# Earlier projections for head pairs and evenly spaced splits of the output weights in a hybrid attention and DeltaNet step

## The chip, the cores and the metric

The kernel runs on one core of one Trainium2 chip. What is compared is the device time of one execution in microseconds (us). The engines are TensorE (PE, matmuls; PEld is its weight load), VectorE (DVE), ScalarE (ACT), GpSimd (POOL) and SyncE (SP), which issues nearly all DMAs here. Each engine works through its own instructions in program order and waits on semaphores for the others.

## What is computed

Two layers of a mixer run over 1280 tokens (256 prompt tokens and 1024 sample tokens) with 1024 features. In each layer one input projection feeds two branches: latent attention with 8 heads, and a gated DeltaNet with 4 heads and one scan per direction. Their gated outputs are joined and go through one output projection. What matters here is the attention branch:

```python
q = jnp.einsum('bsr,rf->bsf', rmsnorm(q_lat, q_a_norm), w_qb)...   # 8 heads of 64 + 32
kv = jnp.einsum('bsr,rf->bsf', ckv_all, w_kvb)...                  # 1536 keys for the sample tokens
s = (jnp.einsum('bqhd,bkhd->bhqk', qn, k_nope)
     + jnp.einsum('bqhr,bkr->bhqk', qp, k_pe)) * scale
p = jax.nn.softmax(s, axis=-1)
o = jnp.einsum('bhqk,bkhd->bqhd', p, v)
...
out = jnp.einsum('bse,ed->bsd', jnp.concatenate([o_a, o_b], axis=-1), w_out)
x = x + gate * out
```

The 256 prompt tokens attend to themselves; the 1024 sample tokens attend to themselves and 256 cached keys.

## The kernel before

**A planner sets the order.** The kernel is written as some forty Python generators ("threads"), each with a priority from the table `PR`. While the kernel is built, `Sched.run` repeatedly takes the operation that can start first by a model of engine clocks and latencies, and among equals the one with the smaller priority number. What it takes is the program order of that engine. A thread stops at `yield "name"` until another thread has set the flag of that name (`sd.flag`), which happens in program order, not in time. Where the model sees PE idle for longer than about a microsecond, `keep_warm` puts in dummy matmuls (line 436, tile `spare`). Nearly all instructions are recorded at one helper line, L315, so they are told apart by their tiles.

**Attention, one layer.** The stage begins while the last DeltaNet heads still run.

- `proj(p)` (p = 0 to 3) makes the queries and keys of heads 2p and 2p+1: three `kp` matmuls of 512 keys, then six `qp` matmuls, all plain fp32. Each result is copied by ACT, its remainder is taken by DVE, and both halves go to DRAM (`kx_d`, `qx_d`). At its end it loads the next pair's weights. Before it begins, it waits for `rest` (the right-hand buffers are open), for `proj{p-1}`, and for tile 5 of head 2p-2.
- `loads(h)` reads head h's keys and queries back from DRAM through SP. Keys have two buffers (`Kt[h % 2]`), so the four pieces wait for tiles 0, 4 and 8 of head h-2 and for its end; queries have three (`Qh[h % 3]`) and wait for the end of head h-3.
- `prep(h)` finds the largest score of each query: 26 `pm` matmuls in two PSUM banks, each reduced by DVE, then a small maximum, a transpose (`mxt`), and a row that goes through DRAM (`mx_d`) into the queries. `pace` holds its parts back to tiles 1 and 6 of head h-2 and tiles 0 and 2 of head h-1.
- `main` works through the heads. For each key tile it issues the score matmuls `sp` (three for 512 queries: high by high, high by low, low by high), ACT takes the exponential into `pe`, and two tiles later `pv` multiplies with the values (`po`). POOL, and for two tiles of a head DVE, adds up the `pe` tiles; one pair of `pd` matmuls makes the denominators from the sum. Head h needs `prep{h}`. The flag `m{h}.{i}` is set when main reaches sample key tile i (0 to 9) of head h, `main{h}` at its end. A head has 66 `sp` matmuls: 6 of 256 columns for the prompt, 60 of 512.
- `vproj(p)` makes the values of a pair (`vp`).

**Output weights.** `pre_c` starts when the last DeltaNet head is done. It loads the output weights in 16 pieces (`wor`, 128 x 512, six buffers), and `split_wo` splits each into a rounded high part (ACT, `woh`) and a remainder (POOL, `wol`). After the last split it opens the pool for the output stage (`load_c`, `mm_thread`, matmuls `wop`), which begins when head 7 has left its prompt block.

Of the kernel before, what the change touches and what calls it, by code (L numbers as in the profile page):

```python
# [16 lines left out]
P = 128  # L17
# [7 lines left out]
NK = T + PAST  # L25
DEPTH = 2
HA = 8
# [370 lines left out]
def body(tc, I, O):  # L398
# [8 lines left out]
    def open_pool(stack, name, bufs=1, **k):  # L407
        return Pool(stack.enter_context(tc.tile_pool(name=name, bufs=bufs, **k)), bufs)
# [8 lines left out]
    def bank(name):  # L417
        yield "bank"
        Sched.banks.remove(min(Sched.banks))
        t = pp.pool.tile([P, 512], F32, tag="mm", name=name)  # L420
        Sched.span(t)
        return t

    def free(t):
        Sched.push(lambda: Sched.banks.append(Sched.after(max(Sched.wr[t.name] + Sched.rd[t.name]), "PE")))
# [138 lines left out]
    def mixer(l, hhl):  # L564
        sd = Sched()
# [803 lines left out]
        def split(x, n):  # L1369

            i = at["evn"] = at.get("evn", -1) + 1
            ev = at["ev"][i % len(at["ev"])]
            S.copy(ev[:, 0, :n], x)
            (V if x.space == PSUM else G).tensor_tensor(ev[:, 1, :n], x, ev[:, 0, :n].bitcast(F32), op=ALU.subtract)
            return ev[:, :, :n].bitcast(F32)

        def proj(p):
            ckv, qn, hw = at["ckv"], at["qn"], at["hw"]
            if p:
                yield "rest"  # L1380
                yield f"proj{p-1}"
                yield f"m{2*p-2}.5"
            for k0 in range(0, NK, 512):
                pt = yield from bank("kp")
                PE.matmul(pt, hw[:, 2, :], ckv[:, k0 : k0 + 512])
                yield 0
                SY.dma_start(kx_d[p, :, :, k0 : k0 + 512], split(pt, 512))
                free(pt)
            for c0, n in BLK:
                pt = yield from bank("qp")  # L1390
                for k in range(2):
                    PE.matmul(pt[:, :n], hw[:, k, :], qn[:, k, c0 : c0 + n], start=(k == 0), stop=(k == 1))
                yield 0
                SY.dma_start(qx_d[p, :, :, c0 : c0 + n], split(pt[:, :n], n))
                free(pt)
            if p + 1 < HA // 2:
                SY.dma_start(hw, I["w_hd"][l, p + 1])
            yield 0
            sd.flag(f"proj{p}")
# [295 lines left out]
        def pre_c():  # L1695
            yield f"done{HB-1}"
            yield "rest"
            gs.close()
            b2 = open_pool(bs, f"b2{l}", bufs=1, side="right")
            for t in ("ob", "rc"):  # L1700
                at[t].append(b2.tile([P, 512], F32, tag=t, name=t))
            cw = open_pool(cs, f"cw{l}", bufs=1)
            xs_ = ExitStack()
            cx = open_pool(xs_, f"cx{l}", bufs=1)
            yield 0
            for e in range(8):
                hi = cw.tile([P, DM], F32R, tag=f"woh{e}", name=f"woh{e}")
                lo = cw.tile([P, DM], F32R, tag=f"wol{e}", name=f"wol{e}")
                wo.append((hi, lo))
                for hf in range(2):  # L1710
                    raw = cx.tile([P, 512], F32, tag="wor", name="wor", bufs=6)
                    sl = slice(hf * 512, hf * 512 + 512)
                    SY.dma_start(raw, I["w_out"][l, e * P : (e + 1) * P, sl])
                    wor.append((hi[:, sl], lo[:, sl], raw))
                    yield 0
                    if len(wor) >= 6:
                        split_wo(wor.pop(0), e)
            while wor:
                split_wo(wor.pop(0), len(wor) // 2)
                yield 0  # L1720
            xs_.close()
            c0 = open_pool(cs, f"c0{l}", bufs=1)
            cc_[0] = c0
            load_gate(0, c0)
            for t in range(2):
                sq[t] = c0.tile([P, 2], F32, tag=f"sq{t}", name="sq")
            sd.add(PR['ldc'], load_c())
            sd.add(PR['mm'], mm_thread())

        wor = []  # L1730

        def split_wo(w, e):
            hi, lo, raw = w
            S.copy(hi, raw)
            (V if len(wor) % 2 < VWO else G).tensor_tensor(lo, raw, hi.bitcast(F32), op=ALU.subtract)
# [14 lines left out]
        def load_c():  # L1750
            for t in range(NT):
                if t == 1:
                    yield f"main{HA-2}"
                    yield f"vv{HA//2-1}"
                    yield f"prep{HA-1}"
                    m1 = at["t1"].rearrange("p (a b) -> p a b", a=4)
                    x, of, cc_["tm"] = m1[:, 0], m1[:, 1].rearrange("p (a b) -> p a b", a=8), m1[:, 2]
                elif t == 2:
                    yield "tm0"
                    yield "C"  # L1760
                if t >= 3:
                    yield f"fin{t-3}"
                if t != 1:
                    x = cc_[0 if t % 3 == 0 else 1].tile([P, DM], F32, tag="x", name="x", bufs=1 if t % 3 == 0 else 2)
                SY.dma_start(x, (I["x"] if l == 0 else xs)[t * P : (t + 1) * P, :])
                if t == 0:
                    yield "attn0"
                    n1 = hp.tile([P, 4, 8, P], F32R, tag="hl1", name="n1")
                pool = cc_.get(t % 2)
                if t != 1:  # L1770
                    of = pool.tile([P, 8, P], F32, tag="of", name="of")
                SY.dma_start(of, o_d[:, :, t * P : (t + 1) * P].rearrange("e p t -> p e t"))
                if t >= 2:
                    yield f"mm{t-2}"
                if t < 2:
                    oh, ol = n1[:, 2 * t], n1[:, 2 * t + 1]
                else:
                    oh, ol = [cc_[1].tile([P, 8, P], F32R, tag=f"o{i}{t%2}", name=f"o{i}") for i in "hl"]
                V.tensor_copy(oh, of)
                G.tensor_tensor(ol, of, oh.bitcast(F32), op=ALU.subtract)  # L1780
                yield 0
                xt[t], ot[t] = x, (oh, ol)
                sd.flag(f"ld{t}")

        def load_gate(t, pool):
            gb[t] = pool.tile([P, DM], F32, tag="gbc", name="gbc", bufs=1)
            SY.dma_start(gb[t], gate_d[l, t // 2 : t // 2 + 1, :].to_broadcast([P, DM]))
# [25 lines left out]
        def mm_thread():  # L1813
            for t in range(NT):
                yield f"ld{t}"
                oh, ol = ot[t]
                x = xt[t]
                if t < 2:
                    s2[t], jk = sq[t], cc_[0].tile([P, 512], mybir.dt.bfloat16, tag="jk", name="jk")
                else:  # L1820
                    s2[t], jk = [cc_[1].tile([P, n], d, tag=f"s{n}", name=f"s{n}", bufs=3 if n == 2 else 1) for n, d in ((2, F32), (512, mybir.dt.bfloat16))]
                for hf in range(2):
                    pt = yield from bank("wop")
                    cs = slice(hf * 512, hf * 512 + 512)
                    for e in range(8):
                        for i, (a, w) in enumerate(((oh, wo[e][0]), (oh, wo[e][1]), (ol, wo[e][0]))):
                            PE.matmul(pt, a[:, e, :], w[:, cs], start=(e == 0 and i == 0), stop=(e == 7 and i == 2))
                        yield 0
                    if t == 1:
                        tm = cc_["tm"][:, cs]  # L1830
                    elif t:
                        tm = cc_[1].tile([P, 512], F32, tag="tm", name="tm", bufs=2)
                    else:
                        tm = cc_[0].tile([P, 512], F32, tag="of", name="tm0")
                    with sd.side(1):
                        V.tensor_tensor(tm, pt, gb[0 if t < 2 else 2][:, cs], op=ALU.mult)
                        free(pt)
                        V.tensor_tensor(x[:, cs], x[:, cs], tm, op=ALU.add)
                        S.activation(jk, x[:, cs], AF.Square, accum_out=s2[t][:, hf : hf + 1])
                        if hf:  # L1840
                            sd.add(PR['fc'], fin(t))
                    if not t and hf:
                        sd.flag("tm0")
                sd.flag(f"mm{t}")
# [124 lines left out]
```

## Time and profile before

| | |
|---|---|
| median of 3 runs | 2251.47 us (2249.32 to 2253.87) |
| the profiled execution | 2246.48 us |
| its span, first to last instruction | 2244.3 us |
| PE busy | 2101.7 us, 94% of the span |
| DVE, POOL, ACT busy | 64%, 38%, 33% of the span |
| mean granted TensorE clock | 0.98 |
| dummy matmuls (`spare`) | 271 instructions, 542 records |

A matmul on plain fp32 leaves two records in the trace, one on the rounded type `fp32r` leaves one. Matmuls overlap in the pipeline, so a record of 0.4 us may begin 0.23 us after the one before; the distance of the starts is what a matmul costs PE. A stretch of the span is named below by its start and end in us. The stretches are cut at the first score matmul of a head, or of a key tile, by counting `sp` records.

### The profile page before, as it was taken

Reading aid. Unit: us, or ns where it says so; the run is one execution under the profiler, and the core shown is the slowest. Engines: PE = TensorE matmul, PEld = TensorE weight load, DVE = VectorE, ACT = ScalarE, POOL = GpSimd, SP = SyncE. Lnnn points to the kernel's source line nnn. Section 1 sums busy time; section 2 is a strip of 40 time slices with the busy share of each in tenths; the row PEclk is TensorE's granted clock in tenths of the full one; section 3 lists DMA queues with packets and bytes.
Section 4 is the critical chain, followed back from the end, with each engine's and each line's share of the span. In section 5 each row is a group of like instructions: output and inputs, shape, how many; then the busy total and the mean of one; then the engine's idle time right before and its main releaser. Section 6 shows DMA issues by size and latency. Waiting matters only on the chain.

```text
span 2244.3 us, 35296 instructions
## 1 busy us (share of the span) xinstructions
PE 2101.7 (94%) x12158; PEld 1570.2 (70%) x12158; DVE 1438.6 (64%) x3105; ACT 739.7 (33%) x2052; POOL 858.1 (38%) x741
## 2 busy tenths in 40 slices
PE   8899999989898998999999999998999899899998
PEld 6677777778575655665777887787876666566586
DVE  4766577775855564563667675987668657456454
ACT  4244224322223344423222441433222333442311
POOL 2343214342414246446331551324252334653721
PEclk9999999999999999999999999999999999999999
DMA  7476777776593736232423655667868573633143
GB/s 272 133 238 186 247 229 223 207 219 217 191 270 120 201 88 183 78 80 62 139 100 94 192 174 153 192 215 211 257 230 244 157 202 88 191 103 79 46 159 108
DMA packets 413091, 380.33 MB, mean 169 GB/s; under 512 B 91585, under 2 KB 334241, under 8 KB 412657
## 3 DMA queue, kind: packets, MB, share of 16 engines
q1 hardware_dynamic: 412912, 378.07, 56.4%
q8 instruction: 97, 1.59, 0.3%
q14 instruction: 82, 0.66, 0.1%
HBM read 246.82 MB, written 131.15 MB: 168 GB/s over the span
## 4 chain that ended last, share of the span: by engine, by line
PE 41%; DVE 15%; DMA 12%; issue 3%; POOL 3%; SPq 3%; ACT 2%; DVEq 0%; POOLq 0%; ACTq 0%
PE wop L315 9%; PE sp L315 7%; PE po L315 6%; PE zp L315 6%; DVE at L315 3%; SPq L315 3%; PE pm L315 2%; DVE wtmp L315 2%; DVE W L315 2%; POOL pe L315 2%; DVE yc L315 2%; DMA at<-kx_d 1%; PE px L315 1%; DMA wr<-in_w_main 1%; DMA qx_d<-at 1%
## 5 line engine op out<-in xcount | busy, mean ns | idle before, releaser
L315 PE MATMUL zp<-hh,wh 128*128 128x512 f32 (+2 forms) x1128 | 423.3, 375 | 10.5 <-DVE wh L315 5.4
L315 PE MATMUL zp<-hl,wh 128*128 128x512 f32 (+2 forms) x1128 | 422.2, 374 | 4.3 <-POOL hl L315 4.2
L315 PE MATMUL zp<-hh,wl 128*128 128x512 f32 (+2 forms) x1128 | 420.8, 373 | 4.7 <-POOL wl L315 4.7
L315 POOL TENSOR_TENSOR pe<-pe,pe 128x1024 f32<-128x1024 f32 x112 | 267.5, 2388 | 283.3 <-PE po L315 213.4
L315 POOL TENSOR_TENSOR wl<-wr,wh 128x512 fp32r<-128x512 f32 (+1 forms) x118 | 161.6, 1371 | 404.8 <-DVE wh L315 231.3
L315 ACT ACTIVATE pe<-sp 128x512 f32<-128x512 f32 (+1 forms) x336 | 196.7, 589 | 216.2 <-PE sp L315 197.9
L315 DVE TENSOR_REDUCE at<-pm 128x1 f32<-128x512 f32 (+1 forms) x336 | 210.1, 682 | 67.3 <-PE pm L315 66.5
L315 PEld LDWEIGHTS zp<-hh,wh 128*128 128x128 f32 (+1 forms) x1128 | 214.7, 190 | 47.7 <-DVE wh L315 6.9
L315 PEld LDWEIGHTS zp<-hl,wh 128*128 128x128 f32 (+1 forms) x1128 | 214.8, 190 | 39.0 <-issue 6.6
L315 PEld LDWEIGHTS zp<-hh,wl 128*128 128x128 f32 (+1 forms) x1128 | 214.4, 190 | 39.3 <-POOL wl L315 7.3
L315 PE MATMUL sp<-at 97*128 97x512 f32 (+1 forms) x572 | 196.3, 400 | 1.2 <-DVE ob L315 0.9
L315 PE MATMUL sp<-at,at 97*128 97x512 f32 (+1 forms) x484 | 186.9, 410 | 1.3 <-ACT vv L315 0.9
L315 PE MATMUL po<-pe,vv 128*64 128x512 f32 (+1 forms) x704 | 163.0, 578 | 0.3 <-ACT pe L315 0.2
L315 POOL TENSOR_SCALAR kpt<-ktok,kdb 128x128 f32<-128x128 f32 x160 | 130.7, 829 | 65.7 <-DMA ai_d<-kpt 55.5
L315 PEld LDWEIGHTS sp<-at 97*128 97x128 f32 x572 | 103.8, 190 | 35.6 <-issue 16.6
L315 DVE TENSOR_TENSOR wtmp<-blk,W 104x31 f32<-104x31 f32 (+15 forms) x248 | 107.2, 432 | 27.5 <-POOL W L315 15.2
L315 PEld LDWEIGHTS sp<-at,at 97*128 97x128 f32 x484 | 91.5, 190 | 34.7 <-issue 11.3
L315 DVE SCALAR_TENSOR_TENSOR yc<-zp_sb,cwh,yc 128x256 f32<-128x256 f32 (+1 forms) x144 | 103.6, 719 | 4.1
L315 PE MATMUL wop<-woh,ol 128*128 128x512 f32 x256 | 101.9, 398 | 1.6 <-POOL ol L315 1.6
L315 PE MATMUL wop<-woh,oh 128*128 128x512 f32 x256 | 102.0, 398 | 0.0
L315 PE MATMUL wop<-wol,oh 128*128 128x512 f32 x256 | 101.9, 398 | 0.0
L315 DVE RECIPROCAL rc<-rc 128x128 f32<-128x128 f32 x80 | 70.0, 920 | 47.7 <-ACT rc L315 47.6
(287 smaller groups left out, 3938.5 us busy)
## 6 DMA issues: line engine op xcount, KB each, us to landing
wr<-in_w_main SPq DMA_DIRECT2D x120, 256.0 KB
ti<-ai_d SPq DMA_DIRECT2D x144, 192.0 KB
ai_d<-ai SPq DMA_DIRECT2D x80, 256.0 KB
kc<-kqv_d SPq DMA_DIRECT2D x160, 128.0 KB
wa<-in_w_ada SPq DMA_DIRECT2D x64, 256.0 KB
kqv_d<-yc SPq DMA_DIRECT2D x48, 256.5 KB
kx_d<-at SPq DMA_DIRECT2D x22, 512.0 KB
kq<-kqv_d SPq DMA_DIRECT2D x16, 641.0 KB
```

The costliest lines, as they stand in the source:

```text
L315: op = Op(lambda: f(*a, **k), self.key, self.ns(name, a, k, aps), outs, [x for x in aps if x is not acc])
```

## The change

`proj(p)` for p = 2 and 3 now waits for tile 0 of head 2p-3 where it waited for tile 5 of head 2p-2, and `proj(1)` waits for no tile at all. `pre_c` waits before each split for a turn: `turn` lists every other key tile of heads 0 to 6, finds at its first call how many of them main has passed, and from there gives one tile to each split.

```diff
@@ -1379,7 +1379,8 @@
             if p:
                 yield "rest"
                 yield f"proj{p-1}"
-                yield f"m{2*p-2}.5"
+                if p > 1:
+                    yield f"m{2*p-3}.0"
             for k0 in range(0, NK, 512):
                 pt = yield from bank("kp")
                 PE.matmul(pt, hw[:, 2, :], ckv[:, k0 : k0 + 512])
@@ -1714,8 +1715,10 @@
                     wor.append((hi[:, sl], lo[:, sl], raw))
                     yield 0
                     if len(wor) >= 6:
+                        yield from turn()
                         split_wo(wor.pop(0), e)
             while wor:
+                yield from turn()
                 split_wo(wor.pop(0), len(wor) // 2)
                 yield 0
             xs_.close()
@@ -1727,7 +1730,16 @@
-        wor = []
+        wor, slots = [], []
+
+        def turn():
+
+            todo = [f"m{h}.{i}" for h in range(HA - 1) for i in range(0, NK // P - 2, 2)]
+            if not slots:
+                slots.append(sum(x in sd.flags for x in todo))
+            i = slots[0]
+            slots[0] += 1
+            yield todo[i] if i < len(todo) else 0
```

Since the flags feed the planner, the order changes over the whole attention stage. The first place is PE in layer 0 around the first score matmul of head 6 (`sp<-at_6431`, 256 columns; `at_7352` and `at_7351` hold head 5's operands, later head 7's). Before:

```order
L315 MATMUL sp<-at_7352 128x512
L315 MATMUL po<-pe,vv 64x512 x2
L315 MATMUL pm<-at_6431 128x512 x2
L315 MATMUL po<-pe,vv 64x512 x2
L315 MATMUL pm<-at_6431 128x512 x14
L315 MATMUL pm<-at_6431 128x256 x8
L436 MATMUL spare<-ident 128x128 x30
L315 MATMUL mxt<-ident,at_6433 10x128
L315 MATMUL pm<-at_7351 128x256 x2
L315 MATMUL pm<-at_7351 128x512 x8
L436 MATMUL spare<-ident 128x128 x6
L315 MATMUL sp<-at_6431 128x256 x2
```

The same place now:

```order
L315 MATMUL sp<-at_7352 128x512
L315 MATMUL sp<-at_6431 128x256 x2
L315 MATMUL sp<-at_6431,at_6432 128x256
L315 MATMUL po<-pe,vv 64x512 x4
L315 MATMUL sp<-at_6431 128x256 x2
L315 MATMUL sp<-at_6431,at_6432 128x256
L315 MATMUL pm<-at_7351 128x512 x2
L315 MATMUL sp<-at_6431 128x512 x2
L315 MATMUL pm<-at_7351 128x512 x2
L315 MATMUL sp<-at_6431,at_6432 128x512
```

All of `prep(6)` (`pm<-at_6431`) and its `mxt` have moved up into heads 4 and 5, `prep(7)` begins among the score matmuls of head 6, and the 36 dummies are gone.

The second place is POOL in layer 0 from head 3 on, where the splits (`wol`) stand among the additions of `pe` and the final products (`ob`). Before:

```order
L315 TENSOR_TENSOR wol_9153<-wor,woh_9152 128x512 x2
L315 TENSOR_TENSOR wol_9161<-wor,woh_9160 128x512 x2
L315 TENSOR_TENSOR pe_9125<-pe_9125,pe 128x1024
L315 TENSOR_TENSOR wol_9171<-wor,woh_9170 128x512 x2
L315 TENSOR_TENSOR ob<-ob,rc 128x512
L315 TENSOR_TENSOR wol_9178<-wor,woh_9177 128x512 x2
L315 TENSOR_TENSOR pe_9125<-pe_9125,pe 128x1024
```

Now:

```order
L315 TENSOR_TENSOR wol_9199<-wor,woh_9198 128x512
L315 TENSOR_TENSOR pe_9203<-pe_9203,pe 128x1024
L315 TENSOR_TENSOR wol_9199<-wor,woh_9198 128x512
L315 TENSOR_TENSOR ob<-ob,rc 128x512
L315 TENSOR_TENSOR pe_9203<-pe_9203,pe 128x1024 x2
L315 TENSOR_TENSOR ob<-ob,rc 128x128
L315 TENSOR_TENSOR wol_9220<-wor,woh_9219 128x512
L315 TENSOR_TENSOR pe_9203<-pe_9203,pe 128x1024
L315 TENSOR_TENSOR wol_9220<-wor,woh_9219 128x512
```

Eight splits stood within two additions; now one or two additions lie between most splits, and the last of the 16 stands in head 6.

The third place is SP in layer 0 where the keys of head 6 are read back (`at_6431<-kx_d`, four pieces). Now loads of raw output weights (`wor`) stand between them:

```order
L315 DMA at_6431<-kx_d 64x256
L315 DMA wor<-in_w_out 128x512 x2
L315 DMA at_6431<-kx_d 64x512
L315 DMA mx_d_5_9649<-at_6433 10x128
L315 DMA wor<-in_w_out 128x512
L315 DMA at_7352<-mx_d_5_9649 1x1280
L315 DMA o_d<-ob 64x512 x2
L315 DMA wor<-in_w_out 128x512
L315 DMA o_d<-ob 64x128 x2
L315 DMA at_6431<-kx_d 64x512
```

Before, all 16 stood ahead of head 4's start, the last of them among the key pieces of heads 4 and 5.

## Rows read from the trace of the kernel before

**Rows 1.** The page's first part: busy us, share of the span, instructions.

```profile
PE 2101.7 (94%) x12158; PEld 1570.2 (70%) x12158; DVE 1438.6 (64%) x3105; ACT 739.7 (33%) x2052; POOL 858.1 (38%) x741
```

**Rows 2.** Busy us (instructions) by stretch: PE, PEld, DVE, ACT, POOL; clock, DMA, GB/s.

```profile
798.00:839.30 41.30, 40.02 (x178) 22.98 (x178) 27.97 (x46) 18.81 (x49) 20.54 (x10) 0.96 0.33 95
...
859.70:888.10 28.40, 25.07 (x110) 16.78 (x110) 14.97 (x22) 11.67 (x22) 24.64 (x16) 0.88 0.64 171
888.10:902.30 14.20, 11.22 (x66) 8.89 (x65) 12.42 (x18) 2.41 (x5) 7.43 (x6) 0.88 0.57 154
...
966.50:989.40 22.90, 21.83 (x116) 15.49 (x116) 16.91 (x28) 1.03 (x3) 0.89 (x1) 0.93 0.36 81
989.40:1017.80 28.40, 28.25 (x134) 17.07 (x133) 16.43 (x26) 12.93 (x24) 17.28 (x9) 1.00 0.14 35
1017.80:1044.80 27.00, 27.00 (x125) 14.99 (x126) 10.29 (x11) 13.70 (x25) 18.94 (x10) 1.00 0.25 69
...
1029.90:1044.80 14.90, 14.90 (x67) 8.14 (x67) 7.24 (x8) 7.51 (x14) 14.03 (x8) 1.00 0.45 125
...
1934.10:1962.80 28.70, 24.59 (x103) 16.09 (x103) 15.44 (x23) 11.05 (x21) 21.49 (x14) 0.88 0.65 177
1962.80:1973.10 10.30, 9.27 (x59) 6.86 (x60) 8.44 (x14) 3.46 (x8) 10.20 (x7) 1.00 0.47 116
...
2038.20:2061.20 23.00, 21.91 (x117) 15.59 (x116) 16.95 (x28) 0.89 (x3) 0.91 (x1) 0.93 0.35 76
```

**Rows 3.** The same for the dummies alone, sum over the six stretches.

```profile
sum 127.50, PE 35.83 PEld 36.20; mean PE 5.97 PEld 6.03
```

**Rows 4.** Timeline between heads 5 and 6, layer 0: start, us, engine, instruction.

```profile
968.08 1.08 PE L315 MATMUL po<-pe,vv 128*64 128x512 f32 x4
...
968.56 12.04 DVE L315 TENSOR_REDUCE at<-pm 128x1 f32<-128x512 f32 x20
...
977.66 7.82 PE L436 MATMUL spare<-ident 128*128 128x128 f32 x60
980.64 0.18 DVE L315 TENSOR_REDUCE at<-at 128x8 f32<-128x24 f32 x1
...
985.32 0.27 PE L315 MATMUL mxt<-ident,at 128*10 128x128 f32 x1
...
989.39 0.49 PE L315 MATMUL sp<-at 97*128 97x256 f32 x2
```

**Rows 5.** Projection 2's query matmuls (min/median/max ns, first to last start); timeline behind.

```profile
L315 PE MATMUL qp<-at,at x12: 377/592/595, 837.7 to 854.0; 128*128 128x512 f32 x8, 128*128 128x256 f32 x4
...
862.25 1.23 SPq L315 DMA_DIRECT2D at<-kx_d  x2
...
867.24 0.77 PE L315 MATMUL pm<-at,at 96*128 96x256 f32 x2 [3.33 <-DMA at<-kx_d]
```

**Rows 6.** Timeline: a maximum matmul between score matmuls, head 3.

```profile
879.60 0.40 PE L315 MATMUL pm<-at,at 96*128 96x512 f32 x1
...
879.83 0.40 PE L315 MATMUL sp<-at,at 97*128 97x512 f32 x1
```

**Rows 7.** First three tiles of head 6 (`pm` alone), and of head 7.

```profile
989.40:1001.70 12.30, 4.41 (x16) 2.73 (x16) 9.29 (x16) 1.00 0.08 24
...
1017.80:1028.40 10.60, 10.60 (x54) 5.61 (x53) 2.25 (x3) 5.06 (x10) 3.49 (x2) 1.00 0.00 0
```

**Rows 8.** The splits of layer 0, DVE's additions, and the timeline where they meet.

```profile
L315 POOL TENSOR_TENSOR wol<-wor,woh x16: 1259/1274/1301, 850.3 to 894.3; 128x512 fp32r<-128x512 f32 x16
...
L315 DVE TENSOR_TENSOR pe<-pe,pe x32: 1161/1224/3357, 716.0 to 2121.7; 128x1024 f32<-128x1024 f32 x32
...
891.82 3.71 POOL L315 TENSOR_TENSOR wol<-wor,woh 128x512 fp32r<-128x512 f32 x3
...
893.44 3.18 DVE L315 TENSOR_TENSOR pe<-pe,pe 128x1024 f32<-128x1024 f32 x1
```

**Rows 9.** SP: two loads of raw output weights, one waiting for its buffer.

```profile
867.96 5.19 SPq L315 DMA_DIRECT2D wor<-in_w_out  x2
```

## The prediction

> **What bounds the kernel now.** First the page's busy line: TensorE (PE) is busy 94% of the span and no other engine over 64% [rows 1]. So the first question is not which engine to relieve but where PE does nothing useful. A busy share hides that here, for two reasons: the planner fills the idle time that it foresees with dummy matmuls (line 436, `spare`), which count as busy, and a matmul that waits in the pipeline counts too. So next I read the busy times by stretch, and the stretches are cut by head: a head's attention is 66 score matmuls (`sp`), counted off in program order.
>
> The reader should look at heads 3 to 7 of layer 0 in that table [rows 2]. Head 7, with nothing beside it, takes 27.0 us with PE at 27.00. Head 6, with 16 maximum matmuls (`pm`) of `prep(7)` beside it, takes 28.4. But between the last score matmul of head 5 and the first of head 6 lie 22.9 us, between heads 3 and 4 lie 14.2 us, and the last six key tiles of head 3 take 28.4 us where the same six of head 7 take 14.9. Layer 1 has the same three stretches: 28.7, 10.3 and 23.0 us [rows 2]. In all six together the dummies alone are 35.83 us [rows 3].
>
> What ends last there is seen in the timeline of the 22.9 us [rows 4]. Main has run dry because head 6 needs `prep(6)`. Its matmuls are issued in one bare run, and VectorE (DVE) takes their maxima 20 in a row, 12.04 us, 0.60 each; then comes the small maximum at 980.64, then `mxt` at 985.32, behind a row of 60 dummy records, then a trip through DRAM, then head 6 at 989.39. `prep(6)` is late because its keys and queries come from projection 3, which starts only at tile 5 of head 4 and ends in head 5. For head 4 it is the same with projection 2: its last matmul starts at 854.0, the first keys are asked for at 862.25, and PE waits 3.33 us for them until 867.24 [rows 5], although the pace that `prep(4)` is allowed (tile 1 of head 2) had passed some 60 us before. So the chain is projection, DRAM and back, bare maxima, maximum row through DRAM, head; and PE pays for it in three places a layer.
>
> **Part 1, the projections.** Nothing is added or removed but the wait's flag: the same 3 `kp` and 6 `qp` matmuls, 6 ACT copies, 6 DVE splits, 6 writes and the weight load for each pair. They stand one head earlier. In the changed order the `pm` of preps 4 to 7 lie between score matmuls, two or so at a time, no bare run is left, and the dummies of heads 3 and 5 are gone: 31 + 36 in layer 0 and 25 + 36 in layer 1, 128 instructions. All other dummies change by -2 in sum (10 fewer around head 0 of layer 0, 8 more ahead of head 0 of layer 1).
>
> What it is worth, stretch by stretch: elapsed time less the useful work in it. A `pm` of 512 columns between score matmuls costs PE 0.23 us (879.60 to 879.83) [rows 6]; of 256 columns I take half, 0.12 (an estimate from the same row); a `po` group of four records at most 1.08 [rows 4].
> - Last six tiles of head 3: 28.4 - 14.9 (head 7's) - 17 pm x 0.23 = 9.6 us. Layer 1: 28.7 - 14.9 - 18 x 0.23 = 9.7.
> - Heads 3 to 4: 14.2 - (9 x 0.23 + 10 x 0.12 + 1.08) = 9.8. Layer 1, 10.3 less the same work but one pm: 6.1.
> - Heads 5 to 6: 22.9 - (24 x 0.23 + 10 x 0.12 + 2 x 1.08) = 14.0. Layer 1: 23.0 less the same, 14.1.
>
> Layer 0 gives 33.4, layer 1 29.9, together 63 us. That is the most these stretches can give if the moved work costs no more than its issue time.
>
> Does it? The good bound: the first three tiles of head 6 with 16 pm took 12.3 us, the same tiles of head 7 without any 10.6 [rows 7]; 1.7 us for 16, 0.11 each, less than I charged. The bad bound is head 2, where everything is mixed (pm, projection 2, the last scan steps): 41.3 us [rows 2]. Its own 27.0, 17 pm (about 3.1), 3 `kp` and 2 `qp` (3.5, at two records of some 0.43 each), and the scan's and gate's small matmuls (about 3) make 36.6; 4.7 us, 11%, is friction. In heads 3 to 6 after the change there are pm and some projection but no scan, so they are nearer to head 6 than to head 2. I take 15% off the 63, 9 us, and keep 0 and 30 us (11% of some 136 us a layer) as ends.
>
> The cover: PE in heads 0 to 2 has the moved projections beside the delta-rule scan, whose chain waits anyway; they are the same matmuls that stood in heads 0, 2 and 4, so heads 1 and 2 get longer by what heads 2 to 5 lose, at nothing in sum. If the scan ends later, the output weights start later; their consumers, the output matmuls, stand behind head 7, some 40 us after the last split.
>
> **Part 2, the splits.** Each layer has 16 pieces: an ACT cast and a POOL subtraction of 1.27 us [rows 8]. Before, they stand in one run from head 3's tile 2 to the gap ahead of head 4. Afterwards there is one for every other key tile from head 3's tile 2 to head 6's tile 4. The work is the same. In the old place they cost something: three splits in a row (891.82, 3.71 us) held DVE's addition at 3.18 us instead of its median 1.22, and the maximum and `mxt` behind it [rows 8]; that is inside the 9.8 above. In the new place: POOL is busy 18.94 us in head 7 [rows 2]; five splits add 6.4, 25.3 in a head of 27 to 34. It fits, with little room. So part 2 alone I put at nothing; its use is that it doesn't fill POOL where the heads now follow at once.
>
> **The sum.** 63 - 9 = 54 us. The profiled execution took 2246.48 us with a span of 2244.3; its span would be 2190. The median of the runs before, 2251.47, lies 5 us above that execution, so 2251.5 - 54 = 2197.
>
> **The rivals.**
> (a) *Mixing costs what it costs in head 2.* DVE is slower than PE at one pm (0.60 a reduction against 0.23), PE's queue is in order, and a pm that finds no free bank stops the score matmuls behind it. For it: head 2's 11%. Against it: head 6's 0.11 us each. At 11% the gain is 63 - 30 = 33, time 2218.
> (b) *The splits collide with DVE on every head.* The row: with splits on POOL DVE's two-input addition at 893.44 ended only after them, at 896.62 [rows 8]. Four last additions a layer stand ahead of the denominator matmul; each held for one or two splits (1.27 to 2.5 us) in both layers is 10 to 20 us: 2212. Against it: POOL's own additions of 2.4 us collide in the same way already. The Trainium skill, "SBUF — State Buffer", section "Who interferes with whom", says that a DVE instruction with two SBUF inputs and a GpSimd one that reads SBUF exclude each other for the whole instruction; this trace agrees, 3.18 us being the rest of the splits and then about 1.1. By that rule spreading the splits spreads the collisions.
> (c) *No change: the keys are late all the same.* K has two buffers, so keys of head h wait for the tiles of head h-2, and the program order says nothing of how long DRAM takes. If the 3.33 us wait of rows 5 grew until PE stood as long as it does now, the time would be 2251. Against it: the order has half a head, some 14 us, between `mxt` of a prep and its head.
> (d) *Slower: the SP queue.* A load of raw output weights waits for a split to free its buffer, and SP is in order. Ten of the 16 loads of a layer now wait for a split that is paced, and the key and query loads of heads 5 and 6 are queued behind them. Before, two such loads held SP 5.19 us [rows 9]. If each held it for a whole pace of two tiles, some 5.5 us, preps would be late by 55 us a layer, against the 32 that is lost now: +23 a layer, 2297. It turns slower from 3.2 us a load. Against it: the load is issued after the split in program order, when the split's own inputs are long there.
>
> **How the numbers follow.** Forecast 2197: chance 0.68. (a) 2218: 0.14. (b) 2212: 0.08. (c) 2251: 0.05. (d) 2297: 0.05. The forecast's own ends are 2181 (all 63 and some of the dummies near head 0) and 2218. The range 2180 to 2221 holds the forecast, (a) and (b), 0.9 less something for errors of size. This kernel's measurement tells about 0.2%, 4.5 us, from no change: faster 0.90, within it 0.05, slower 0.05.
>
> **What would show it.** Right: no dummies between heads 1 and 7; the gap between heads 3 and 4 and between 5 and 6 under 1 us in both layers; heads 3 to 7 at 27 to 38 us each; one split at a time on POOL, and no PE wait over 2 us for `at<-kx_d`. Rival (a) shows as PE waits of pm on DVE and heads at 33 us and more without projections; (b) as DVE additions of 3 us beside `wol`, and `pd` waiting on them; (d) as SP rows of `wor` of 3 us and more with pm waiting on `kx_d` behind. The prediction is wrong if the gaps close and the time doesn't fall with them: then the work that I counted at issue price costs more where it now stands.

## The result, and the profile after

| | before | after |
|---|---|---|
| median | 2252.67 us (2249.32 to 2258.53) | 2193.11 us (2190.5 to 2197.3) |
| the profiled execution's span | 2244.3 us | 2191.2 us |

The ratio is 0.9735, 95% interval 0.9709 to 0.9761: 59.6 us less by these medians. Forecast were 2197, in a range of 2180 to 2221.

The busy line, which answers to [rows 1], says as little as before: PE stays at 94%.

```profile
PE 2057.0 (94%) x11898; PEld 1534.6 (70%) x11898; DVE 1438.4 (66%) x3105; ACT 734.7 (34%) x2052; POOL 853.5 (39%) x741
```

The stretches show it. These are heads 3 to 7 of layer 0 and then head 3 of layer 1, each from its first score matmul to the next head's (columns as in [rows 2]), and behind them the dummies alone between heads 1 and 7 of either layer.

```profile
834.60:881.10 46.50, 42.35 (x170) 23.75 (x170) 25.24 (x39) 17.77 (x35) 20.59 (x12) 0.93 0.58 171
881.10:913.30 32.20, 31.77 (x150) 19.43 (x149) 20.69 (x32) 15.72 (x31) 24.22 (x14) 1.00 0.47 118
913.30:947.70 34.40, 34.40 (x175) 22.22 (x173) 21.66 (x32) 17.58 (x34) 24.62 (x16) 1.00 0.34 80
947.70:978.10 30.40, 30.29 (x141) 17.53 (x140) 15.92 (x23) 14.75 (x28) 24.68 (x13) 1.00 0.39 100
978.10:1005.00 26.90, 26.90 (x125) 14.93 (x125) 10.04 (x11) 13.59 (x25) 18.75 (x10) 1.00 0.24 68
1891.20:1937.40 46.20, 42.57 (x170) 23.94 (x169) 25.38 (x39) 17.70 (x36) 20.50 (x12) 0.93 0.58 172
```

```profile
733.00:1005.00 272.00, 0.00 (x0) 0.00 (x0) 0.99 0.46 125
1786.70:2061.40 274.70, 0.00 (x0) 0.00 (x0) 0.99 0.45 123
```

The heads follow each other without a gap, the dummies of [rows 3] are gone, and heads 4 to 7 run at full clock with PE busy nearly all the time. One head stands out in both layers: head 3, 46 us long, with PE idle or slow for part of it.

The span alone is a poor ruler for such parts. The stretch ahead of projection 0 has the same program order in all kernels here and still took 569 to 581 us. So I compare stages, cut by matmuls in the trace: the start of the first `kp` of projection 0, the start of the first `sp` of head 3, and the end of the last `sp` of head 7, in us ("to head 3" thus holds the stretch ahead of head 0 too):

| kernel | L0: to head 3 | heads 3–7 | L1: to head 3 | heads 3–7 | both stages |
|---|---|---|---|---|---|
| before | 265.1 | 205.4 | 262.0 | 203.0 | 935.5 |
| after | 263.9 | 170.3 | 271.0 | 170.0 | 875.3 |
| part 1 alone | 262.2 | 174.5 | 272.7 | 174.5 | 883.9 |
| part 2 alone | 261.4 | 193.6 | 264.3 | 196.7 | 916.0 |
| part 2 and projection 3 | 265.7 | 190.8 | 260.1 | 194.4 | 911.0 |
| projection 1 alone | 260.1 | 211.3 | 261.3 | 207.5 | 940.2 |
| after, projection 1 late | 276.9 | 167.8 | 273.7 | 171.5 | 889.9 |
| after, loads behind projection 3 | 263.2 | 165.6 | 270.9 | 165.7 | 865.4 |
| part 1, run behind projection 3 | 264.7 | 168.2 | 272.1 | 168.6 | 873.5 |

Before to after is 60.2 us in the two stages, which agrees with the medians. The two profiled spans are only 53.1 us apart: outside the stages the profiled execution of the changed kernel took 7 us longer, above all between the layers (615.2 us from the end of layer 0's head 7 to layer 1's first `kp`, against 606.6 before and 606.4 to 612.5 in the other kernels here). Whether the change has a part in that isn't shown.

### The profile page after: what moved, and what is told of

The parts are those of the page before. It is cut to its first block, busy times and chain, and to the rows that moved or that the text cites. A ratio compares the mean times of both kernels' runs of the same rounds, so it can differ in the third digit from the quotient of the medians.

```text
span 2191.2 us, 34803 instructions
## 1 busy us (share of the span) xinstructions
PE 2057.0 (94%) x11898; PEld 1534.6 (70%) x11898; DVE 1438.4 (66%) x3105; ACT 734.7 (34%) x2052; POOL 853.5 (39%) x741
## 4 chain that ended last, share of the span: by engine, by line
PE 49%; DVE 12%; DMA 7%; POOL 3%; issue 3%; ACT 2%; SPq 1%; POOLq 0%; DVEq 0%; ACTq 0%
PE zp L315 10%; PE sp L315 8%; PE wop L315 8%; PE po L315 8%; PE pm L315 3%; DVE wtmp L315 2%; POOL pe L315 2%; DVE W L315 2%; PE px L315 1%; SPq L315 1%; PE up L315 1%; DVE at L315 1%; PE qp L315 1%; DMA kx_d<-at 1%; PE ks L315 1%
## 5 line engine op out<-in xcount | busy, mean ns | idle before, releaser
L315 PE MATMUL sp<-at,at 97*128 97x512 f32 (+1 forms) x484 | 179.9, 398 | 6.8 <-ACT pe L315 6.8
L315 POOL TENSOR_SCALAR kpt<-ktok,kdb 128x128 f32<-128x128 f32 x160 | 124.8, 792 | 67.7 <-DMA ai_d<-kpt 56.3
L315 DVE CAST wh<-wr 128x512 fp32r<-128x512 f32 (+1 forms) x122 | 59.3, 487 | 63.9 <-DMA wr<-in_w_main 36.0
```

What stands on the lines that cost most here:

```text
L315: op = Op(lambda: f(*a, **k), self.key, self.ns(name, a, k, aps), outs, [x for x in aps if x is not acc])
```

## Which part does it

Part 1 alone, the edit against the kernel before (the splits stay in one run):

```diff
-                yield f"m{2*p-2}.5"
+                if p > 1:
+                    yield f"m{2*p-3}.0"
```

> Part 1 alone: the projections' new flags, the splits of the output weights in one run as before. Theory A (the prediction: the late projections are the cause of the three gaps a layer, part 2 adds nothing): the gaps between heads 3 and 4 and between 5 and 6 are gone, time 2193 to 2200 us. Theory B (a run of 16 splits on POOL and ACT now hits heads that follow at once, so part 2 is needed): the exponentials of heads 3 and 4 wait for additions on POOL, some 10 us a layer, time 2210 to 2220 us.

Measured 2201.41 us (2197.04 to 2202.34), ratio 0.9774 [0.9739, 0.9808], 1 us above theory A's range and 9 below theory B's. Part 1 brings 51 of the 60 us.

Part 2 alone (before, with the turns):

> Part 2 alone: splits in turns, the projections at their old flags. Theory A (the prediction): the projections are as late as before, the gaps stay, time 2247 to 2257 us. Theory C (the run of 16 splits with its loads, on ACT, POOL and SP, was itself a cause of the gaps: of 128 dummies in heads 3 and 5 the program order keeps 44 here): the gap between heads 5 and 6 shrinks to under 10 us, time 2215 to 2230 us.

Measured 2233.23 us (2226.33 to 2236.16), ratio 0.9915 [0.9887, 0.9943]. So part 2 alone is worth 19 us, where the prediction had nothing, but on top of part 1 only 8 (2201.41 to 2193.11; the intervals of the two ratios overlap, the stages give 8.6). The stretches of this kernel between heads 3 and 4, head 5 itself, and between heads 5 and 6:

```profile
880.50:889.30 8.80, 6.68 (x36) 4.12 (x35) 7.97 (x13) 0.86 (x2) 1.49 (x1) 1.00 0.55 128
920.50:964.00 43.50, 40.84 (x183) 24.44 (x183) 23.16 (x33) 18.87 (x35) 25.71 (x16) 0.96 0.43 112
964.00:972.00 8.00, 6.20 (x31) 3.64 (x32) 7.81 (x13) 0.86 (x2) 1.44 (x1) 1.00 0.50 123
```

The gaps of 14.2 and 22.9 us [rows 2] fall to 8.8 and 8.0, while head 5 grows from 34.1 to 43.5.

The run of splits stood in the same late chain as the projections, though hardly in projection 2 itself: from its first `kp` to the first read of head 4's keys are 39.5 us in the kernel before (822.75 to 862.25) and 37.8 here (817.82 to 855.61). From that read to head 4's `mxt` are 34.5 us before (to 896.75) and 26.7 here (to 882.35). In between, the reads of further keys stand behind loads of output weights on SP, and these wait for splits. What SP waited for the splits from 840 to 905 us, before and then here (us in all, times, longest):

```profile
SPq L315 <- POOL wol L315: 13.6, 5, 5.0
```

```profile
SPq L315 <- POOL wol L315: 8.5, 5, 2.9
```

DVE's additions beside the splits are in that stretch too (3.18 us, [rows 8]). How much of the 7.8 us each has isn't shown. Either part shortens this one chain, so the one that is made first earns most of it.

Do the gaps add up? Part 2 with projection 3 alone begun sooner (the edit against the kernel with part 2 alone):

```diff
-                yield f"m{2*p-2}.5"
+                yield f"m{2*p-2}.5" if p < 3 else f"m{2*p-3}.0"
```

> The changed kernel with projections 1 and 2 back at their old flags; only projection 3 is early, and the splits are in turns. Theory A (each projection pays for the gap that stands behind it): the gap between heads 5 and 6 is gone, worth 14 us a layer, the 9.6 + 9.8 us around head 3 stay, time 2220 to 2228 us. Theory C (the gap behind heads 3 comes from the run of splits): both are gone, 2195 to 2210 us.

Measured 2223.18 us (2216.99 to 2227.88), ratio 0.9873 [0.9834, 0.9911]. The time lies in theory A's range by luck, for its account is wrong: the gap ahead of head 6 is gone, but the one ahead of head 4 doesn't stay, it grows from 8.8 to 22.0 us (22.3 in layer 1). Between heads 3 and 4, and SP in that gap:

```profile
890.00:912.00 22.00, 19.88 (x99) 14.47 (x99) 11.71 (x19) 1.99 (x5) 0.02 (x1) 0.84 0.50 141
```

```profile
896.13 5.04 SPq L315 DMA_DIRECT2D qx_d<-at  x2
901.27 0.49 SPq L315 DMA_DIRECT2D mx_d<-at  x1
```

Projection 2 is still late, and projection 3 now ends in the same place: of `prep(4)` 9 `pm` are left there, of `prep(5)` 10 stand there already, and among them projection 3's last query matmuls. On SP head 4's row of maxima (`mx_d`) goes out behind projection 3's last query write. From `mxt` (897.06) to head 4 (912.02) it takes 15.0 us, where the kernel before takes 5.5 (896.75 to 902.28). So closing one gap alone moved the wait to the other.

## Projection 1, which I had at nothing

Projection 1 alone begun sooner, and then the reverse, the changed kernel with projection 1 late:

```diff
-                yield f"m{2*p-2}.5"
+                if p > 1:
+                    yield f"m{2*p-2}.5"
```

> The kernel before with projection 1 alone begun early, projections 2 and 3 and the splits as before. Theory H (projection 1's copies and splits stand among prep(1)'s reductions and delay head 1, and in layer 0 PE has idle time ahead of head 0 to take them): heads 0 to 2 of layer 0 shorten by 8 to 12 us, layer 1 by 0 to 4, the gaps behind heads 3 and 5 stay, time 2238 to 2244 us. Theory A (the prediction: no gain in sum): 2249 to 2256 us.

```diff
-                if p > 1:
-                    yield f"m{2*p-3}.0"
+                yield f"m{2*p-2}.5" if p < 2 else f"m{2*p-3}.0"
```

> The changed kernel with projection 1 alone back at its old flag (tile 5 of head 0). Theory A (the prediction: moving projection 1 is worth nothing in sum): 2190 to 2198 us. Rival: projection 1 fills PE where the scan of layer 0 makes it wait (heads 0 to 2 lost 39.6 us before and 32.1 after in layer 0): its move is worth about 7 us, time 2198 to 2204 us.

Alone: 2250.85 us (2246.37 to 2258.6), ratio 0.9986 [0.9965, 1.0008], no change. Missing from the others: 2213.35 us (2210.2 to 2218.3), ratio 0.9833 [0.9796, 0.9869], 20 us slower than with it and outside both ranges. The same edit is worth nothing alone and 20 us with the others (14.6 by the stages). In the first kernel the stretches to head 3 are 5.0 and 0.7 us shorter, and heads 3 to 7 give it back, in layer 0 in the gaps behind heads 3 and 5, which both grow (14.2 and 22.9 before, [rows 2]):

```profile
885.90:903.30 17.40, 12.55 (x73) 10.29 (x73) 15.01 (x18) 2.93 (x6) 9.54 (x7) 0.80 0.52 140
967.50:991.70 24.20, 23.32 (x115) 17.02 (x115) 16.85 (x28) 0.93 (x3) 0.93 (x1) 0.86 0.34 76
```

In the second one, the gap between heads 0 and 1 stays and head 1 grows; the stretches are that gap and head 1 of layer 0, with projection 1 late and then as changed:

```profile
733.60:749.30 15.70, 13.84 (x81) 9.42 (x79) 6.81 (x17) 4.16 (x14) 0.00 (x0) 1.00 0.83 254
749.30:814.90 65.60, 61.06 (x344) 44.21 (x344) 41.80 (x96) 23.31 (x60) 18.27 (x9) 1.00 0.57 161
```

```profile
725.20:733.70 8.50, 8.28 (x53) 5.59 (x52) 6.38 (x10) 2.40 (x5) 3.58 (x2) 1.00 0.84 194
733.70:790.50 56.80, 55.03 (x297) 38.31 (x298) 37.09 (x83) 21.83 (x56) 17.89 (x9) 1.00 0.64 187
```

81.3 against 65.3 us: 16 in layer 0, of which 10.5 are left over the whole stage (444.7 against 434.2; 4.2 in layer 1). In layer 1 the gap is 14.1 us (1785.2 to 1799.3, last and first `sp`) against none. Head 1 has 344 matmul records against 297, among them 10 more `pm`, 16 more `vp` and 14 of dummies: projection 1 stands in head 0 there, and these `pm` and `vp`, which the changed kernel has in head 0, come behind it, into the head that has projection 2 too.

## What holds head 3

Here the prediction's rival (d) is found, at one place a layer. SP in head 3 of the changed kernel, in order (start, us, engine, operation):

```profile
838.82 0.53 SPq L315 DMA_DIRECT2D o_d<-gt  x1
843.97 0.34 SPq L315 DMA_DIRECT2D wor<-in_w_out  x1
844.40 0.45 SPq L315 DMA_DIRECT2D at<-kx_d  x1
844.91 2.48 SPq L315 DMA_DIRECT2D wor<-in_w_out  x5
847.43 0.57 SPq L315 DMA_DIRECT2D kx_d<-at  x1
```

What SP waited for before that first load (836 to 850 us; us in all, times, longest):

```profile
SPq L315 <- DMA o_d<-gt: 4.6, 1, 4.6
```

ACT, DVE and PE at the same time, with the idle time ahead of an instruction in brackets, ACT at the same place of layer 1, and a stretch of the windows view:

```profile
839.65 0.59 ACT L315 CAST at<-kp 128x512 fp32r<-128x512 f32 x1 [1.59 <-PE kp L315]
...
847.20 0.62 ACT L315 CAST woh<-wor 128x512 fp32r<-128x512 f32 x1 [5.32 <-DMA at<-kx_d]
...
854.56 0.58 ACT L315 CAST at<-kp 128x512 fp32r<-128x512 f32 x1 [3.85 <-DMA kx_d<-at]
```

```profile
840.50 0.68 DVE L315 TENSOR_TENSOR at<-kp,at 128x512 fp32r<-128x512 f32 x1
```

```profile
848.37 0.79 PE L315 MATMUL sp<-at,at 97*128 97x512 f32 x1 [3.14 <-ACT pe L315]
```

```profile
1904.36 0.62 ACT L315 CAST woh<-wor 128x512 fp32r<-128x512 f32 x1 [5.81 <-DMA wor<-in_w_out]
```

```profile
848.40:858.10 9.70, 8.69 (x24) 3.67 (x25) 2.93 (x5) 3.19 (x6) 3.22 (x3) 0.69 0.66 216
```

The first load of a raw output weight waits on SP until 843.97; the pool that it is taken from is opened where the one with the gate (`gt`) was closed, and the gate's last write was issued at 838.82. Five more loads follow, and projection 3's first key write, whose two halves were ready at 841.18 (DVE's row), goes out at 847.43. ACT first idles 5.32 us ahead of the cast of the first weight piece; the profile puts that down to a load of the same queue, and in layer 1, where it is 5.81 us, to the weight load itself. The exponentials stand behind that cast, and PE waits 3.14 us for them. Then ACT's next projection cast waits 3.85 us for the key write, since the pieces share one buffer (`ev`), with more exponentials behind it. Over the 9.7 us behind its wait PE's granted clock is 0.69, a mean of its two levels, 1.2 and 2.4 GHz. In part 1 alone the longest PE wait of head 3 is 6.8 us, in layer 1 of the changed kernel 3.6.

A first try, the turns one place later, on the theory that the first splits are in the way:

```diff
-                slots.append(sum(x in sd.flags for x in todo))
+                slots.append(sum(x in sd.flags for x in todo) + 1)
```

> The changed kernel, but every split one turn (two key tiles) later. In the changed kernel ACT's first cast of an output weight stands at head 3's third tile and waits for its load to land; the exponentials behind it are late, PE waits 3.1 us in layer 0 and 3.6 in layer 1 for them, and the clock granted after that is 0.69 and 0.62 of full for some 9 us. Theory F (that cast is the cause): both waits go, head 3 falls from 46.5 and 46.2 us to 40 to 43, time 2180 to 2188 us. Theory G (ACT would wait there for projection 3's write to DRAM anyway): the wait changes its name, 2190 to 2196 us.

Measured 2194.49 us (2190.83 to 2202.4), ratio 0.9752 [0.9725, 0.978]: no gain, and head 3 is no shorter (47.5 and 49.3 us, 46.5 and 46.2 in the changed kernel). The wait only changed its name, in layer 0 to 5.7 us of `pd` for ACT:

```profile
PE pd L315 <- ACT pe L315: 5.7, 1, 5.7
```

```profile
846.38 0.34 SPq L315 DMA_DIRECT2D wor<-in_w_out  x1
...
847.31 3.01 SPq L315 DMA_DIRECT2D wor<-in_w_out  x5
850.37 0.57 SPq L315 DMA_DIRECT2D kx_d<-at  x1
```

The turns pace the splits; the six loads ahead of the first split are issued as before, and the key write stands behind them as before. So the loads themselves were moved behind projection 3:

```diff
             cx = open_pool(xs_, f"cx{l}", bufs=1)
-            yield 0
+            yield f"proj{HA//2-1}"
```

> The changed kernel with one edit: the six loads of output weights, which enter SP's queue ahead of projection 3's first key write (843.97 to 847.4 us, the write at 847.43, though its cast was done at 839.65), wait in the program until projection 3 is done. Theory G (head 3's loss is this queue): the write goes out near 840, ScalarE's second cast of projection 3 doesn't wait for it, TensorE's wait of 3.1 us in the tile of sums behind it and the half-clocked stretch after it go, head 3 falls from 46.5 to some 40 us in both layers, stages of 434 and 441 become 428 and 435: 2180 to 2187 us. Theory L (the loads only change places): the splits, which now run from head 4 to the start of head 7, are late for the output stage or meet preparation work in heads 4 to 6, which grow by as much: 2190 to 2197 us.

Measured 2181.3 us (2178.57 to 2183.56), ratio 0.9675 [0.965, 0.9701]: 12 us less than the change. Its head 3, then SP's first key write there, whose cast began at 847.46:

```profile
842.40:884.60 42.20, 41.44 (x186) 24.58 (x186) 24.75 (x39) 16.55 (x31) 17.95 (x9) 1.00 0.47 141
```

```profile
849.16 0.57 SPq L315 DMA_DIRECT2D kx_d<-at  x1
```

From cast to write it is 1.70 us, where it was 7.78 (839.65 to 847.43), and the next projection cast begins 3.93 us behind the write (853.09) where it was 7.13; no PE wait over 0.7 us is left between heads 3 and 7, the clock is 1.00, and heads 3 to 7 take 165.6 and 165.7 us. Head 3 fell from 46.5 to 42.2 us, not quite to the 40 that theory G gave it, and 8 dummies stand in it in each layer. The splits, now as late as the start of head 7, cost nothing that shows.

That leaves a question on part 2: is it the spacing of the splits that helps, or their place? Part 1 alone, with its run of loads and splits put behind projection 3 and no turns:

> The kernel with part 1 alone (projections sooner, output weights split in one run as before), and that run put behind projection 3 in the program, without the pacing of part 2. Theory Q (what part 2 brings is the place of the loads and splits, not their spacing): the wait of 6.8 us that TensorE has in head 3 of part 1 alone goes, heads 3 to 7 fall from 174.5 to 167 us a layer or less, as in the kernel with the loads behind projection 3 and the pacing (165.6 and 165.7): 2180 to 2188 us. Theory R (the spacing itself is needed): 16 casts and splits in one block hold ScalarE's exponentials and VectorE's additions in heads 4 and 5, which are 4 to 8 us a layer longer than with pacing, heads 3 to 7 take 170 us and more: 2189 to 2200 us.

Measured 2187.04 us (2182.86 to 2190.65), ratio 0.9718 [0.9694, 0.9742]. Its heads 3 to 5 of layer 0:

```profile
833.80:876.00 42.20, 41.43 (x186) 24.63 (x185) 24.81 (x39) 16.14 (x31) 15.89 (x8) 1.00 0.48 140
876.00:909.10 33.10, 32.75 (x151) 19.44 (x151) 21.90 (x32) 18.36 (x36) 25.14 (x17) 1.00 0.61 170
909.10:944.60 35.50, 34.83 (x174) 22.19 (x173) 22.36 (x32) 18.36 (x35) 31.23 (x18) 1.00 0.44 116
```

The wait of 6.8 us is gone (the longest in head 3 is 0.7). The time lies in theory Q's range, the heads (168.2 and 168.6 us) between the two. Both are true in part: the place is worth 6 us a layer (174.5 to 168.4, mean of the layers), the spacing on top of it 3 (to 165.7), which is in heads 4 and 5. One line changed in `pre_c` does at least as much as part 2 as it was built: heads 3 to 7 take 168.4 against 170.2 us a layer, while the intervals of the two kernels' ratios overlap.

## Where POOL and DVE meet

Rival (b) is found too, at the end of head 7 in either layer. The changed kernel, layer 0:

```profile
1010.00 2.35 POOL L315 TENSOR_TENSOR n<-at,n 128x1024 fp32r<-128x1024 f32 x1
1010.08 3.36 DVE L315 TENSOR_TENSOR pe<-pe,pe 128x1024 f32<-128x1024 f32 x1 [2.28 <-POOL pe L315]
...
1013.49 1.08 PE L315 MATMUL pd<-pe,twos 128*64 128x512 f32 x4 [2.85 <-DVE pe L315]
```

POOL's remainder of the second output tile starts 0.08 us ahead of DVE's last addition, which then takes 3.36 us in place of its median 1.23, and PE waits 2.85 us for it. In layer 1 this is no work of the change: the kernel before has the same there (below), and a PE wait of 2.91 us. First I gave the remainder a planner's flag behind that addition:

```diff
+                            if last:
+                                sd.flag(f"la{b['h']}.{b['c0']}")
...
+                if t == 1:
+                    yield f"la{HA-1}.{SEQ}"
```

> The changed kernel, but POOL's remainder of the second output tile is issued after DVE's last addition of head 7. In the changed kernel POOL started it 0.07 to 0.08 us before DVE's addition in both layers, the addition took 3.36 us in place of 1.2, and PE waited 2.85 us for the denominators, with a granted clock of 0.69 behind it. Theory P (the two exclude each other, whoever starts first): DVE's addition takes 1.2 us, PE's wait falls under 1 us, 2 to 4 us a layer, time 2185 to 2190 us. Rival: the output matmuls of the second tile now wait for POOL, 2192 to 2196 us.

Measured 2193.21 us (2185.84 to 2198.2), ratio 0.9743 [0.9715, 0.9771]. It tested nothing: the flag orders the program, not the time, and on another engine POOL started at the same moment (PE waits 2.8 us as before). With the shift of the turns added:

> Both of the last two edits together. If they are independent their gains add: by theories F and P 2172 to 2184 us; by their rivals 2190 to 2196 us.

Measured 2199.65 us (2195.88 to 2203.08), ratio 0.9771 [0.9745, 0.9798], no gain either, as follows from its two halves. Its head 3 takes 49.2 and 50.0 us; why it is longer than with the shift alone isn't shown. On DVE the order is real, since DVE works in program order, so the remainder went there (the flag is set as above):

```diff
...
-                G.tensor_tensor(ol, of, oh.bitcast(F32), op=ALU.subtract)
+                if t == 1:
+                    yield f"la{HA-1}.{SEQ}"
+                (V if t == 1 else G).tensor_tensor(ol, of, oh.bitcast(F32), op=ALU.subtract)
```

> The changed kernel with one edit: POOL's remainder of the second output weight tile, which starts 0.08 us before VectorE's last addition of head 7 (1010.00 and 1010.08), is done by VectorE behind that addition. Theory P (the addition of two SBUF tiles is slow because POOL works beside it): it takes some 1.2 us in place of 3.36, TensorE's wait for it falls from 2.85 to under 1 us in both layers, the output stage shortens by 2 to 4 us a layer: 2185 to 2190 us. Rival: the remainder on VectorE delays what follows there, and TensorE waits for that as long as before: 2192 to 2196 us.

Measured 2186.06 us (2185.48 to 2189.07), ratio 0.97 [0.9675, 0.9725]. The same place:

```profile
1016.45 1.23 DVE L315 TENSOR_TENSOR pe<-pe,pe 128x1024 f32<-128x1024 f32 x1 [2.28 <-POOL pe L315]
1017.60 1.22 DVE L315 TENSOR_TENSOR n<-at,n 128x1024 fp32r<-128x1024 f32 x1
...
1017.73 1.08 PE L315 MATMUL pd<-pe,twos 128*64 128x512 f32 x4 [0.71 <-DVE pe L315]
```

1.23 us, as theory P had it, and a PE wait of 0.71; layer 1 shows 1.23 and 0.72. The stretch behind head 7 of layer 1 to the end of the span took 125.9 us, in both kernels with this edit, against 129.9 in the changed kernel and 126.9 to 129.9 in all others, so at least 1 us of it is the edit's. The Trainium skill, "SBUF — State Buffer", section "Who interferes with whom", says that a DVE instruction with two SBUF inputs contends with a GpSimd one that reads SBUF; these rows agree, 2.35 us of POOL's and then some 1.1 of its own being the 3.36.

Both edits together:

> The changed kernel with both edits, loads of output weights behind projection 3 and the second tile's remainder on VectorE behind the last addition of head 7. If both theories hold their gains lie in different stages and add: 2173 to 2182 us. If only one holds, the time of that one, 2180 to 2190; if neither, 2190 to 2197.

Measured 2179.26 us (2170.72 to 2185.36), ratio 0.9654 [0.9626, 0.9681]. It is the fastest kernel here by its median, and its stages and its end are those of the two apart (heads 3 to 7 165.8 and 165.7, end 125.9), but from the loads alone, 2181.3, the times don't tell it.

## Why the prediction was right, point by point

**The bound and its place.** Right. PE's lost time lay behind heads 3 and 5 and in the end of head 3, and it came back there: heads 3 to 7 take 35.1 and 33.0 us less, 68 together, where the sum had 63 as the most. They gave up more than was counted, since work left them for the heads ahead: without dummies 751 matmul records start in them in layer 0, where it was 793 (24 `vp`, 10 `pm` and 8 `qp` fewer).

**Heads 0 to 2 "at nothing in sum".** Right by size, wrong by reason. From the start of head 0 to that of head 3 it is 148.8 us before and 149.1 after in layer 0, 149.6 and 148.4 in layer 1. But that is a balance: the gap between heads 0 and 1 fell from 15.4 and 14.4 us (730.8 to 746.2 and 1804.2 to 1818.6, last and first `sp`) to 8.5 and 0, and the three heads themselves grew by about as much (head 1 of layer 0, start to start, from 51.7 to 59.4). I had no term for that gap. Nor had I one for the stretch ahead of head 0, where projection 1's keys now stand: from projection 0's first `kp` to head 0 it fell by 1.5 us in layer 0 and grew by 10.3 in layer 1 (112.4 to 122.7), which is the +9.0 of the stage to head 3 there. The run with projection 1 late, where the gap stays, shows what hangs on it.

**Friction, 15% or 9 us.** The net of the stages is 60.2 of 63, so 3 us, less than I took, and not where I looked. I spread the friction evenly over the mixed heads, and they ran freely: head 6 at 30.4 and head 4 at 32.2 us. Head 5, at 34.4, is above the 33 that I gave as a sign of rival (a), but PE is busy in it throughout, with 24 `vp` that I hadn't placed there, and no PE wait for DVE between heads 3 and 7 is over 0.6 us. So (a) did not come. What was lost sat in head 3, a queue and not a mixing cost: moving the loads gave 10 us back in the stages (875.3 to 865.4). With them the stages give 70.1 us, more than the 63 that I called the most. That the time came within 4 us of the forecast is in part luck, a balance of terms that I didn't have: the gap between heads 0 and 1 and 5 us more in heads 3 to 7 on one side, layer 1's stretch ahead of head 0 and head 3's queue on the other.

**Part 2 "alone I put at nothing".** The step that failed. It is 19 us alone and 8 on top of part 1. I had priced the splits' delay of DVE (3.18 us, [rows 8]) and counted it inside the gap, but not that its loads hold SP in front of head 4's keys as well (five waits for splits, 13.6 us in all), though [rows 9] showed one such wait. Part 1 brought 51 of the 54 us forecast, part 2's 8 are the rest and the excess.

**The rivals.** (c) did not come: between heads 1 and 7 PE waits for no key load. (d) came in another shape. I looked for paced loads holding the keys of heads 5 and 6. SP does wait for splits there, 12.0 us in seven waits with 3.3 as the longest (850 to 960 us), but no PE wait comes of it. What held were the first six, of which the first waits for memory and not for a split, and what they held was a write. (b) came at a POOL operation that is not a split, for 2.85 us a layer, of which layer 1's was there before. Beside a split one DVE addition a layer took 2.09 us (918.51 and 1974.90), and no PE wait over 0.6 us followed.

**What would show it.** No dummies between heads 1 and 7, the gaps, and splits one at a time (`wol` x16 from 847.9 to 954.7 us) came as written. Heads "27 to 38 us each" failed for head 3.

## What to carry to other kernels

Gaps that look separate can be one chain: price an edit with the rest of the change in place as well as alone, since here one move was worth 0 or 20 us (15 by the stages), another 19 or 8. When work is moved forward, read each in-order queue from the place it leaves to the place it lands, and ask of a load into freed memory what it waits for and which write stands behind it. A flag of a planner orders the program only; to keep two engines apart in time, put the work on the engine whose order does it.

## What the runs showed of the hardware

Less than two tenths of a microsecond decides over 2 us. In the kernel before, layer 0, DVE's addition came 0.16 us first and POOL's subtraction paid (3.30 us for 2.35), with a PE wait of 0.71; after, POOL came 0.08 us sooner and DVE paid 3.36 for 1.23, with PE behind it. In layer 1 of the kernel before, POOL (2121.62) was 0.07 us sooner already. The kernel before, layers 0 and 1:

```profile
1049.88 1.21 DVE L315 TENSOR_TENSOR pe<-pe,pe 128x1024 f32<-128x1024 f32 x1
1050.04 3.30 POOL L315 TENSOR_TENSOR n<-at,n 128x1024 fp32r<-128x1024 f32 x1 [0.63 <-DVE n L315]
...
2121.69 3.36 DVE L315 TENSOR_TENSOR pe<-pe,pe 128x1024 f32<-128x1024 f32 x1 [2.30 <-POOL pe L315]
```

And a short PE wait cost more here than it lasted. Behind the 2.85 us wait in the output stage the granted clock was 0.69 from 1014.5 to 1020.0, as over the 9.7 us behind the 3.14 us in head 3; with the wait at 0.71 us the same place keeps 1.00. By the two rows below, 19 matmul records took 5.50 us at 0.69, and at the other row's 25 in 5.26 they would take 4.0: an estimate of 1.5 us on top of the 2.85. The changed kernel, then the one with the remainder on DVE:

```profile
1014.50:1020.00 5.50, 5.50 (x19) 4.35 (x18) 3.89 (x5) 0.58 (x1) 0.00 (x0) 0.69 0.00 0
```

```profile
1018.74:1024.00 5.26, 5.26 (x25) 4.26 (x24) 5.20 (x8) 0.59 (x1) 0.41 (x1) 1.00 0.00 0
```
